# One-bank PSUM tiles, a sum moved past the meeting of the MLP halves, and accumulating output stores in a hybrid block on Trainium2

## The chip, the cores and the metric

The kernel runs on one core of one Trainium2 chip. Its time is the device time of one execution in microseconds; the median of three executions of the kernel before is 2062.95 us (2062.31 to 2064.06).

## The reference

One layer of a streaming encoder for 512 tokens of width 2048, in float32. Cut to what matters:

```python
h = rmsnorm(x, norm_mix_pre)
proj = h @ w_in                                  # 2048 -> 1024 + 4 * 1024: u, q, f, i, g
y_pool = pool_mixer(u, pool_w, pool_b, pool_scale)
y_hgrn = hgrn2_mixer(q, f, i, g, lb, hgrn_norm_w)    # gated linear recurrence, chunks of 64
mix = concatenate([y_pool, y_hgrn]) @ w_out      # 2048 -> 2048
x = x + rmsnorm(mix, norm_mix_post)
h = rmsnorm(x, norm_mlp_pre)
ff = square(relu(h @ w_mlp_in)) @ w_mlp_out      # 2048 -> 8192 -> 2048
x = x + rmsnorm(ff, norm_mlp_post)
```

## The kernel before

**Products.** Each float32 operand is split into a high part (a ScalarE cast to a shorter format, names with h: wh, mh) and a low part (a VectorE subtraction, names with l: wl, ml; lines L214, L215 for the projections' weights, L857, L858 for the MLP's, L1124, L1125 for its activations). Each product is three matmuls: high by high, high by low, low by high. A bank of PSUM holds 128 partitions by 512 float32; there are eight.

**Order.** The program is written out by hand. On each engine the instructions run in the order in which the Python code issues them; a pool of tiles or a data dependence adds a wait to an instruction, but nothing is reordered. Dependences in PSUM are kept by tile: where two banks are one tile, an instruction that writes the second bank is ordered behind one that reads the first.

**Input projection and w_out (L250).** The projection runs in ten groups, each filling four banks, and w_out in four groups (n = 0 to 3, 512 columns each) with the four row tiles of 128 tokens as its four banks. The depth of 2048 is done in four units; in the last unit each bank is finished in turn and then evicted, that is, read out of PSUM and scaled, by VectorE (pu L436, F L515, Q L534) or ScalarE (V L541, G L546); for w_out by ScalarE's square with a row sum (junk L810) and VectorE's product with a gain (Y L811). The recurrence runs between, in small pieces handed out by a clock of units; it uses the other four banks (pool pss). The residual task after w_out makes the rows x2 = x + rmsnorm(mix) of each row tile t, and stores them from POOL's queue into a DRAM buffer x2_dram.

**MLP.** It is a Strassen-type scheme: 16 groups g, each with seven products i in the order (1, 2, 5, 3, 6, 7, 4), and each product in two column blocks q: 14 slots in a group, 224 in all. Groups 0 to 7 are the in half (products_in: L1019 with 256 columns in g = 0, while the pool pss is still open and four banks are left; L1014 and L1015 after that, with eight). Slots of the in half are evicted by evac_in in two parts h: take (ScalarE copy L1052) and add (VectorE L1049, L1067) collect products in a buffer t, which finish_in multiplies by the row factor and squares (L1033, L1034) and stores to h_dram (L1035, POOL's queue). Groups 8 to 15 are the out half (products, L1208); evac_out adds each slot's bank pair to the rows YT (L1233).

**The meeting of the halves.** The activations of the out half are read back into r and combined: act_steps lists sums S (sum_a, L1132) and splits (split_a, L1124, L1125) with the slot before which each is to be ready, and run_pend pops them in this order, some in each slot. S and the buffers t of the last in group come from one pool tag, "tmp", with three buffers, so a new S waits until the store of an old t has read its buffer.

**Queues.** SP's queue carries plain weight loads, the loads of r, the residual rows xs and the output stores (L1260). POOL's queue carries the weight loads that accumulate two blocks into one tile (L864), the stores to h_dram and those of x2.

**End.** In the last group, d counts its 14 slots. At d = 4 the four row tiles of x2 are loaded back as xs. Slots with the last product of a column block are added (L1233), squared with a row sum (L1240, ScalarE), multiplied by the gain wpost (L1246, VectorE); finish_steps then makes y · rt + xs (L1258) for each row tile in three steps and stores it. Steps of the row tiles 0 and 1 are popped two per slot from d = 9 on; those of 2 and 3 stand in the last slot, which is evicted in two halves.

Of the kernel before, what the change touches and what calls it, by code (L numbers as in the profile page):

```python
# [28 lines left out]
def hybrid_block(  # L29
# [34 lines left out]
    psg = ctx.enter_context(tc.tile_pool(name="psg", bufs=2, space=PSUM))  # L64
# [699 lines left out]
    def residual_task(t):  # L764
# [10 lines left out]
        nc.gpsimd.dma_start(x2_dram[t * P:(t + 1) * P, :], Y[t])  # L775
# [182 lines left out]
    ps_in = [psg.tile([P, 2, 512], F32, tag="g", name=f"mi{k}") for k in range(2)]  # L958
    PA, PG = ps_in[0:1], ps_in[1:2]
# [38 lines left out]
    def products_in(k, hook):  # L998
# [9 lines left out]
        for n, (m, kt) in enumerate(mk):  # L1008
# [7 lines left out]
            else:  # L1016
                o = main[0][:, m // 2, (m % 2) * 256:(m % 2) * 256 + 256]
# [117 lines left out]
    def act_steps(p):  # L1135
# [7 lines left out]
            (0, 0, lambda: sum_a(1, None, r_block(1, 1), ALU.subtract)),  # L1143
# [22 lines left out]
    for k in range(n_in):  # L1166
# [21 lines left out]
        if k == 13:  # L1188
            assert "rbc2" in late
            pss_pool.__exit__(None, None, None)  # L1190
            psm = ctx.enter_context(tc.tile_pool(name="psm", bufs=1, space=PSUM, reuse_waits="tile"))
# [4 lines left out]
    al, ga = ps_mo, ps_in[::-1]

    def products(k):
# [6 lines left out]
        for h, kt in hk:  # L1205
            ts = slice(h * P, (h + 1) * P)
            for oi, (l, r) in enumerate(((0, hi), (0, lo), (1, hi))):
                nc.tensor.matmul(bank[:, h, :], a[:, l, kt, ts], r[:, kt, :],  # L1208
# [10 lines left out]
    def evac_out(k):  # L1219
# [10 lines left out]
        end = k == len(slots) - 1  # L1230
        parts = [slice(h, h + 1) for h in range(2)] if end else [slice(0, 2)]
        for hs in parts:
            nc.vector.tensor_tensor(out=yv[:, hs], in0=yv[:, hs], in1=bank[:, hs],  # L1233
                                    op=ALU.add if sign > 0 else ALU.subtract)
# [6 lines left out]
            if end:  # L1241
                yw = M["yw"][:, hs]
            else:
                yw = yv
# [1 line left out]
            nc.vector.tensor_tensor(out=yw if end else yw[:, hs], in0=yv[:, hs], in1=wp, op=ALU.mult)  # L1246
# [73 lines left out]
```

## Time and profile before

| | us |
|---|---|
| median of 3 runs | 2062.95 (2062.31 to 2064.06) |
| profiled execution | 2061.68 |
| its span | 2060.0 |
| PE busy | 1975.7 (96%) |
| VectorE busy | 1286.0 (62%) |
| ScalarE busy | 832.7 (40%) |
| POOL busy | 195.6 (9%) |
| HBM traffic | 326.14 MB read, 25.17 MB written, 171 GB/s |

The stages on the span: input projection with the recurrence until about 546 us, w_out until 745, the in half of the MLP until about 1430, the out half to the end. The page's rows name an engine, a line and "out<-in" tiles: pj are the projection's banks, om those of w_out, mi and mo those of the MLP. A bracket [0.79 <-DVE F L515] says that the engine had been idle for 0.79 us and that VectorE's F at L515 ended the wait.

### The profile page before, as it was taken

To read this page: it belongs to the slowest core of one execution; us is meant where nothing else is said; L and a number is where in the kernel's file an instruction comes from. 1 tells how busy PE (TensorE), PEld (TensorE's weight loads), DVE (VectorE), ACT (ScalarE), POOL (GpSimd) and SP (SyncE) were. 2 spreads that over 40 slices of the span, in tenths; PEclk is the share of its full clock that TensorE was granted. 3 is DMA by queue.
4 is the path that set the end of the run, shared out by engine and by line. 5 is a ranking of instruction groups with operands and counts; after the bars stand their busy time and mean duration, and the time that the engine had idled before them with its cause. 6 is when DMAs were issued, how large, how long until landed. Compare 5 with 4: busy or idle time off the path is not lost.

```text
span 2060.0 us, 24502 instructions
## 1 busy us (share of the span) xinstructions
PE 1975.7 (96%) x10066; PEld 1665.3 (81%) x10066; DVE 1286.0 (62%) x1392; ACT 832.7 (40%) x1009; POOL 195.6 (9%) x229
## 2 busy tenths in 40 slices
PE   9999999999989987999999999998999999999995
PEld 7778887888777777888888888887888888888884
DVE  4537533653632267566666656666778778778877
ACT  5322222222232255444444444445554444444443
POOL 1000000000000001011111111110110110110110
PEclk9999999999999998999999999999999999999998
DMA  5322123221243276798998998996998998998994
GB/s 193 104 82 82 62 82 98 68 80 62 93 183 102 82 215 112 213 206 210 209 215 211 216 212 215 217 245 172 252 222 205 236 222 213 222 227 219 224 241 127
DMA packets 165680, 352.90 MB, mean 171 GB/s; under 512 B 6008, under 2 KB 9152, under 8 KB 163776
## 3 DMA queue, kind: packets, MB, share of 16 engines
q0 software_dynamic: 73680, 160.47, 40.2%
q1 hardware_dynamic: 91888, 190.86, 27.1%
q8 instruction: 79, 1.29, 0.3%
q14 instruction: 33, 0.27, 0.0%
HBM read 326.14 MB, written 25.17 MB: 171 GB/s over the span
## 4 chain that ended last, share of the span: by engine, by line
PE 88%; DVE 5%; ACT 2%; issue 1%; DMA 0%; DVEq 0%; ACTq 0%; POOLq 0%
PE pj L250 20%; PE mo L1208 16%; PE mi L1208 13%; PE mi L1014 9%; PE om L250 8%; PE mo L1014 8%; PE mi L1015 5%; PE mo L1015 4%; PE mi L1019 3%; PE lps L600 2%; DVE ml L858 1%; DVE t L1049 1%; ACT mh L857 0%; DVE YT L1258 0%; PE po L663 0%
## 5 line engine op out<-in xcount | busy, mean ns | idle before, releaser
L1014 PE MATMUL mi<-a,mh 128*128 128x512 f32 x896 | 316.5, 398 | 11.9 <-DVE t L1049 11.9
L1208 PE MATMUL mo<-mh,o 128*128 128x512 f32 x1024 | 318.5, 391 | 1.1 <-ACT mh L857 1.1
L250 PE MATMUL pj<-xT,wh 128*128 128x512 f32 x768 | 243.3, 397 | 10.9 <-DVE pu L436 3.8
L858 DVE TENSOR_TENSOR ml<-X,mh 128x1024 fp32r<-128x1024 f32 x176 | 207.4, 1220 | 70.3 <-ACT mh L857 70.3
L1015 PE MATMUL mi<-a,ml 128*128 128x256 f32 x896 | 251.1, 280 | 0.0
L857 ACT CAST mh<-X 128x1024 fp32r<-128x1024 f32 x176 | 179.7, 1050 | 167.8 <-PE mo L1014 53.4
L1208 PE MATMUL mi<-mh,o 128*128 128x512 f32 x768 | 237.7, 389 | 0.0
L858 DVE TENSOR_TENSOR ml<-YX,mh 128x1024 fp32r<-128x1024 f32 x176 | 207.4, 1220 | 46.1 <-ACT mh L857 46.1
L857 ACT CAST mh<-YX 128x1024 fp32r<-128x1024 f32 x176 | 180.1, 1051 | 137.8 <-PE mo L1208 48.0
L1014 PE MATMUL mo<-a,mh 128*128 128x512 f32 x672 | 235.2, 395 | 0.0
L1208 PEld LDWEIGHTS mo<-mh,o 128*128 128x128 f32 x1024 | 192.9, 188 | 42.2 <-ACT mh L857 2.2
L215 DVE TENSOR_TENSOR wl<-wr,wh 128x1024 fp32r<-128x1024 f32 (+1 forms) x116 | 136.2, 1186 | 132.8 <-ACT wh L214 132.6
L1014 PEld LDWEIGHTS mi<-a,mh 128*128 128x128 f32 x896 | 169.3, 189 | 53.7 <-ACT mh L857 7.3
L1208 PE MATMUL mo<-ml,o 128*128 128x512 f32 x512 | 200.3, 391 | 6.4 <-DVE ml L858 6.4
L1015 PE MATMUL mo<-a,ml 128*128 128x256 f32 x672 | 187.5, 279 | 0.0
L250 PEld LDWEIGHTS pj<-xT,wh 128*128 128x128 f32 x768 | 142.0, 189 | 45.4 <-DVE pu L436 5.5
L214 ACT CAST wh<-wr 128x1024 fp32r<-128x1024 f32 (+1 forms) x116 | 115.3, 1016 | 156.4 <-PE pj L250 81.8
L250 PE MATMUL pj<-wh,xT 128*128 128x512 f32 x512 | 170.0, 398 | 3.1 <-ACT G L546 3.1
L1015 PEld LDWEIGHTS mi<-a,ml 128*128 128x128 f32 x896 | 170.0, 190 | 0.0
L1208 PEld LDWEIGHTS mi<-mh,o 128*128 128x128 f32 x768 | 144.1, 188 | 29.9
L250 PE MATMUL pj<-xT,wl 128*128 128x512 f32 x384 | 150.5, 392 | 0.0
L1014 PEld LDWEIGHTS mo<-a,mh 128*128 128x128 f32 x672 | 126.1, 188 | 30.0
(222 smaller groups left out, 3033.0 us busy)
## 6 DMA issues: line engine op xcount, KB each, us to landing
wr<-in_w_in SPq DMA_DIRECT2D x39, 1024.0 KB, 5.2
X<-in_w_mlp_in POOLq DMA_DIRECT2D x33, 1024.0 KB, 8.7
X<-in_w_mlp_out POOLq DMA_DIRECT2D x33, 1024.0 KB, 9.8
YX<-in_w_mlp_in POOLq DMA_DIRECT2D x23, 1024.0 KB, 9.8
YX<-in_w_mlp_out POOLq DMA_DIRECT2D x23, 1024.0 KB, 9.8
YX<-in_w_mlp_in SPq DMA_DIRECT2D x21, 1024.0 KB, 5.4
YX<-in_w_mlp_out SPq DMA_DIRECT2D x21, 1024.0 KB, 5.1
wr<-in_w_out SPq DMA_DIRECT2D x16, 1024.0 KB, 5.1
```

The lines of the kernel that those rows point to most:

```text
L214: nc.scalar.copy(out=hi[:, ks, :], in_=raw[:, ks, :])
L215: nc.vector.tensor_tensor(out=lo[:, ks, :], in0=raw[:, ks, :], in1=hi[:, ks, :].bitcast(F32), op=ALU.subtract)
L250: nc.tensor.matmul(bank, l, r, start=first and kt == 0 and oi == 0, stop=last and kt == 3 and oi == 2)
L600: nc.tensor.matmul(ps[r:r + mb, h, w, b0:b1], K[:, h, w * P + r:w * P + r + mb], rhs[:, b0:b1, 1, :], start=True, stop=True)
L857: nc.scalar.copy(out=hi[:, ks, :], in_=raw[:, ks, :])
L858: nc.vector.tensor_tensor(out=lo[:, ks, :], in0=raw[:, ks, :], in1=hi[:, ks, :].bitcast(F32), op=ALU.subtract)
L1014: nc.tensor.matmul(o, hi[:, kt, ms], r, start=st, stop=False, skip_group_check=True)
L1015: nc.tensor.matmul(o[:, 0], lo[:, kt, ms], r[:, 0], start=False, stop=sp, skip_group_check=True)
L1019: nc.tensor.matmul(o, l[:, kt, ms], r[:, x], start=st and oi == 0 and m % 2 == 0, stop=sp and oi == 2, skip_group_check=True)
L1049: nc.vector.tensor_tensor(out=t, in0=t, in1=half(banks, s_), op=sign)
L1208: nc.tensor.matmul(bank[:, h, :], a[:, l, kt, ts], r[:, kt, :], start=i in (1, 2, 5) and kt == 0 and oi == 0, stop=kt == 3 and oi == 2, sk ...
```

## The change

Four edits.

1. The pool psg gives four tiles of one bank instead of two of two banks. This holds for the projection, w_out and the first group of the MLP (g = 0).
2. When the recurrence's pool closes (slot 13), psg closes with it and a new pool psm takes all eight banks as four two-bank tiles; at the meeting psm closes, and a pool pso takes them as al0, ga0, ga1 (two banks each) and al1 as two one-bank tiles. A slot in al1 (i in 1, 6, 7, 4 with q = 1) is evicted by two operations of 512 columns instead of one of 1024.
3. For the first out group (p = 0) the sum S1 may run only from the end of the in half on (14 instead of 0 in the table of act_steps); the entries behind it follow, since the list is popped in order.
4. The rows x2 of the row tiles 0 and 1 are stored to the output itself instead of x2_dram. They are not loaded again; their finish is y · rt · wpost (one operation, 1024 columns each time) and a store from POOL's queue that accumulates into the output. The separate product with wpost goes for them. Their four steps are popped at d = 10, 11 and 12 and, the last, inside the last slot between its two halves.

The core of the diff:

```diff
-    psg = ctx.enter_context(tc.tile_pool(name="psg", bufs=2, space=PSUM))
+    psg_pool = tc.tile_pool(name="psg", bufs=4, space=PSUM)
+    psg = psg_pool.__enter__()
...
     def new_banks(name):
-        g = [psg.tile([P, 2, 512], F32, tag="g", name=f"{name}_{j}") for j in range(2)]
-        return [g[j // 2][:, j % 2] for j in range(4)]
+        return [psg.tile([P, 512], F32, tag="g", name=f"{name}_{j}") for j in range(4)]
...
-        nc.gpsimd.dma_start(x2_dram[t * P:(t + 1) * P, :], Y[t])
+        nc.gpsimd.dma_start((out2d if t < 2 else x2_dram)[t * P:(t + 1) * P, :], Y[t])
...
-    ps_in = [psg.tile([P, 2, 512], F32, tag="g", name=f"mi{k}") for k in range(2)]
-    PA, PG = ps_in[0:1], ps_in[1:2]
+    ps_in = [psg.tile([P, 512], F32, tag="g", name=f"mi{k}") for k in range(4)]
+    PA, PG = ps_in[0:2], ps_in[2:4]
...
-                o = main[0][:, m // 2, (m % 2) * 256:(m % 2) * 256 + 256]
+                o = main[m // 2][:, (m % 2) * 256:(m % 2) * 256 + 256]
...
-            (0, 0, lambda: sum_a(1, None, r_block(1, 1), ALU.subtract)),
+            (0, 0 if p else 14, lambda: sum_a(1, None, r_block(1, 1), ALU.subtract)),
...
             pss_pool.__exit__(None, None, None)
-            psm = ctx.enter_context(tc.tile_pool(name="psm", bufs=1, space=PSUM, reuse_waits="tile"))
-            ps_mo = [psm.tile([P, 2, 512], F32, name=f"mo{q}") for q in range(2)]
-            PA, PG = ps_in[::-1], ps_mo
+            psg_pool.__exit__(None, None, None)
+            psm_pool = tc.tile_pool(name="psm", bufs=1, space=PSUM, reuse_waits="tile")
+            psm = psm_pool.__enter__()
+            ps_in = [psm.tile([P, 2, 512], F32, name=f"ps{q}") for q in range(4)]
+            PA, PG = ps_in[2:4], ps_in[0:2]
     while ends:
         ends.pop(0)()
-    al, ga = ps_mo, ps_in[::-1]
+    psm_pool.__exit__(None, None, None)
+    pso = ctx.enter_context(tc.tile_pool(name="pso", bufs=1, space=PSUM, reuse_waits="tile"))
+    al = [pso.tile([P, 2, 512], F32, name="al0")] + [[pso.tile([P, 512], F32, name=f"al1{h}") for h in range(2)]]
+    ga = [pso.tile([P, 2, 512], F32, name=f"ga{q}") for q in range(2)]
...
-        parts = [slice(h, h + 1) for h in range(2)] if end else [slice(0, 2)]
-        for hs in parts:
-            nc.vector.tensor_tensor(out=yv[:, hs], in0=yv[:, hs], in1=bank[:, hs],
-                                    op=ALU.add if sign > 0 else ALU.subtract)
+        op = ALU.add if sign > 0 else ALU.subtract
+        for hs in [slice(h, h + 1) for h in range(2)] if type(bank) is list else [slice(0, 2)]:
+            src = bank[hs.start].unsqueeze(1) if type(bank) is list else bank
+            if g == NP and i in FIRST:
+                nc.scalar.copy(out=yv[:, hs], in_=src)
+                continue
+            nc.vector.tensor_tensor(out=yv[:, hs], in0=yv[:, hs], in1=src, op=op)
...
-            wp = M["wpost"][:, cs].unsqueeze(1).to_broadcast([P, hs.stop - hs.start, 512])
-            nc.vector.tensor_tensor(out=yw if end else yw[:, hs], in0=yv[:, hs], in1=wp, op=ALU.mult)
+            if tp == 2:
+                yw = M["yw"][:, hs] if end else yv[:, hs]
+                wp = M["wpost"][:, cs].unsqueeze(1).to_broadcast([P, hs.stop - hs.start, 512])
+                nc.vector.tensor_tensor(out=yw, in0=yv[:, hs], in1=wp, op=ALU.mult)
             if end:
                 for f in finish_steps(2 + hs.start):
                     f()
+                while steps:
+                    steps.pop(0)()
...
+            if t < 2:
+                nc.vector.scalar_tensor_tensor(out=y[:, c0:c1], in0=y[:, c0:c1], scalar=rt[0],
+                                               in1=M["wpost"][:, c0:c1], op0=ALU.mult, op1=ALU.mult)
+                nc.gpsimd.dma_start(out2d[rows, c0:c1], y[:, c0:c1], accum_op=ALU.add)
+                return
...
-            xa, xb = M["r"], M["12"].bitcast(F32)
-            for t in range(4):
-                load_xs(t, flat((xa if t < 2 else xb)[:, t % 2]))
+            for t in (2, 3):
+                load_xs(t, flat(M["r"][:, t % 2]))
...
-        for _ in range(2):
-            if steps and d < 13:
-                steps.pop(0)()
+        elif 10 <= d <= 12:
+            steps.pop(0)()
```

How the order moves. First TensorE in the last unit of w_out's group n = 0, from the last matmul of the first row tile's bank into the second's; wh and wl are the split weights, mp the split activations, and om_0 before is the tile that holds the banks of the row tiles 0 and 1. Before:

```order
L250 MATMUL om_0_3552<-wh_3720,mp_3675 128x512 [waits Activation_49]
L250 MATMUL om_0_3552<-wl_3721,mp_3675 128x512
L250 MATMUL om_0_3552<-wh_3720,mp_3675 128x512 [waits DVE_49] x2
L250 MATMUL om_0_3552<-wl_3721,mp_3675 128x512
L250 MATMUL om_0_3552<-wh_3720,mp_3675 128x512 x2
```

And now:

```order
L251 MATMUL om_0_3572<-wh_3742,mp_3697 128x512 [waits Activation_49]
L251 MATMUL om_0_3572<-wl_3743,mp_3697 128x512
L251 MATMUL om_0_3572<-wh_3742,mp_3697 128x512 [waits DVE_49]
L251 MATMUL om_1_3573<-wh_3742,mp_3697 128x512
L251 MATMUL om_1_3573<-wl_3743,mp_3697 128x512
L251 MATMUL om_1_3573<-wh_3742,mp_3697 128x512 x2
```

Before, two matmuls with a wait for VectorE stand side by side: the last of the first bank, and the first of the second bank. Now the second bank is a tile of its own, om_1, and its first matmul has no wait.

VectorE at the meeting of the halves; t_ is the buffer of a product of the last in group (t_9389, t_9228, t_9565 before; t_9422, t_9261, t_9593 now), S_9457 or S_9656 the sum S1, ml a low part of split weights. Before:

```order
L1033 SCALAR_TENSOR_TENSOR t_9389<-t_9389,rbc 128x1024 [waits DVE_49]
L1132 TENSOR_TENSOR S_9457<-S_9366,r 128x1024 [waits DMASW4_49,Activation_49]
L858 TENSOR_TENSOR ml_4644<-YX,mh_4643 128x1024 [waits DMASW2_49,PE_49,Activation_49]
L858 TENSOR_TENSOR ml_4644<-YX,mh_4643 128x1024 [waits PE_49,Activation_49]
L1049 TENSOR_TENSOR t_9228<-t_9228,mi_4685 128x512 [waits PE_49]
```

And now:

```order
L1033 SCALAR_TENSOR_TENSOR t_9422<-t_9422,rbc 128x1024 [waits DVE_49]
L858 TENSOR_TENSOR ml_4672<-YX,mh_4671 128x1024 [waits DMASW2_49,PE_49,Activation_49]
L858 TENSOR_TENSOR ml_4672<-YX,mh_4671 128x1024 [waits PE_49,Activation_49]
L1049 TENSOR_TENSOR t_9261<-t_9261,ps_5662 128x512 [waits PE_49]
...
L1033 SCALAR_TENSOR_TENSOR t_9593<-t_9593,rbc 128x1024 [waits DVE_49]
L858 TENSOR_TENSOR ml_4711<-YX,mh_4710 128x1024 [waits DMAHW2_49,Activation_49]
L858 TENSOR_TENSOR ml_4711<-YX,mh_4710 128x1024 [waits Activation_49]
L1132 TENSOR_TENSOR S_9656<-S_9399,r 128x1024 [waits DMASW5_49]
```

S1, with its wait for a DMA, stood between the finish of one t and the additions to the next; it now stands behind the finish of the last t.

VectorE in the last two slots; YT_9328 before and YT_9361 now hold the row tiles 0 and 1, YT_9416 and YT_9449 the tiles 2 and 3, YX the gain wpost. Before:

```order
L858 TENSOR_TENSOR ml_4683<-X_4470,mh_4682 128x1024 x2
L1233 TENSOR_TENSOR YT_9416<-YT_9416,mo_5629 128x2x512
L1246 TENSOR_TENSOR YT_9416<-YT_9416,YX 128x2x512
L1233 TENSOR_TENSOR YT_9416<-YT_9416,mo_5630 128x512
L1246 TENSOR_TENSOR yw<-YT_9416,YX 128x512
```

And now, from the same add of slot d = 12:

```order
L1239 TENSOR_TENSOR YT_9449<-YT_9449,al_9622 128x2x512
L1249 TENSOR_TENSOR YT_9449<-YT_9449,YX 128x2x512
L753 TENSOR_REDUCE sst<-ss_m 128x1
L134 TENSOR_SCALAR msq<-sst 128x1
L756 RECIPROCAL rt_y<-rt_y 128x1
L757 SCALAR_TENSOR_TENSOR rt<-rt_y,msq 128x1
L758 SCALAR_TENSOR_TENSOR rt<-rt,rt_y 128x1
L1264 SCALAR_TENSOR_TENSOR YT_9361<-YT_9361,rt,YX 128x1024
L1239 TENSOR_TENSOR YT_9449<-YT_9449,al_9623 128x512
L1249 TENSOR_TENSOR yw<-YT_9449,YX 128x512
```

The beginning of row tile 1's finish, its row factor (L753 to L758) and its first 1024 columns, stood two slots earlier before; it now stands between the last full eviction and the first half of the last slot. Its second 1024 columns stand still later, between the two halves of the last slot.

More of the change, by code (lines that the diff above doesn't have):

```diff
@@ L1042, in half @@
             if s_ is None:
-                return banks[0][:, h].rearrange("p (a b) -> p a b", a=2)
+                return banks[h].rearrange("p (a b) -> p a b", a=2)
             return banks[h][:, :, s_ * 256:(s_ + 1) * 256]
@@ L1207, in products @@
             for oi, (l, r) in enumerate(((0, hi), (0, lo), (1, hi))):
-                nc.tensor.matmul(bank[:, h, :], a[:, l, kt, ts], r[:, kt, :],
+                nc.tensor.matmul(bank[h] if type(bank) is list else bank[:, h, :], a[:, l, kt, ts], r[:, kt, :],
                                  start=i in (1, 2, 5) and kt == 0 and oi == 0,
@@ L1225, in evac_out @@
         yv = M["y1" if tp == 1 else "y2"][:, :, cs]
-        if g == NP and i in FIRST:
-            nc.scalar.copy(out=yv, in_=bank)
-            return
         final = g == 2 * NP - 1 and i in LAST
         end = k == len(slots) - 1
-        parts = [slice(h, h + 1) for h in range(2)] if end else [slice(0, 2)]
-        for hs in parts:
-            nc.vector.tensor_tensor(out=yv[:, hs], in0=yv[:, hs], in1=bank[:, hs],
-                                    op=ALU.add if sign > 0 else ALU.subtract)
+        op = ALU.add if sign > 0 else ALU.subtract
[5 more added lines that the diff above has]
+            nc.vector.tensor_tensor(out=yv[:, hs], in0=yv[:, hs], in1=src, op=op)
             if not final:
@@ L1240, in evac_out @@
                 nc.scalar.activation(out=junk, in_=yv[:, h], func=AF.Square, accum_out=ss_m[:, t, n:n + 1])
[L1241 to L1244, printed above, removed]
-            wp = M["wpost"][:, cs].unsqueeze(1).to_broadcast([P, hs.stop - hs.start, 512])
-            nc.vector.tensor_tensor(out=yw if end else yw[:, hs], in0=yv[:, hs], in1=wp, op=ALU.mult)
+            if tp == 2:
+                yw = M["yw"][:, hs] if end else yv[:, hs]
+                wp = M["wpost"][:, cs].unsqueeze(1).to_broadcast([P, hs.stop - hs.start, 512])
+                nc.vector.tensor_tensor(out=yw, in0=yv[:, hs], in1=wp, op=ALU.mult)
             if end:
@@ L1254, in finish_steps, with begin @@
         y = y_rows(t)
+        rows = slice(t * P, (t + 1) * P)
         def part(c0, c1):
-            src = M["yw"][:, t % 2] if t >= 2 and c0 == 1024 else y[:, c0:c1]
+            if t < 2:
[3 more added lines that the diff above has]
+                return
+            src = M["yw"][:, t % 2] if c0 == 1024 else y[:, c0:c1]
             nc.vector.scalar_tensor_tensor(out=y[:, c0:c1], in0=src, scalar=rt[0], in1=M["xs", t][:, c0:c1],
                                            op0=ALU.mult, op1=ALU.add)
-            nc.sync.dma_start(out2d[t * P:(t + 1) * P, c0:c1], y[:, c0:c1])
-        return [lambda: (rt.append(row_rstd(t)), part(0, 1024)), lambda: part(1024, 1536), lambda: part(1536, 2048)]
+            nc.sync.dma_start(out2d[rows, c0:c1], y[:, c0:c1])
+        def begin():
+            rt.append(row_rstd(t))
+            part(0, 1024)
+        if t < 2:
+            return [begin, lambda: part(1024, 2048)]
+        return [begin, lambda: part(1024, 1536), lambda: part(1536, 2048)]
     def load_xs(t, tl):
```

## The prediction

> **What bounds the kernel now.** I read the page's busy shares and its chain of waits first, then TensorE's waits by releaser, then a table of the span by stage, then the timeline at the waits that are worth something.
>
> ```profile
> span 2060.0 us, 24502 instructions
> PE 1975.7 (96%) x10066; PEld 1665.3 (81%) x10066; DVE 1286.0 (62%) x1392; ACT 832.7 (40%) x1009; POOL 195.6 (9%) x229
> PE 88%; DVE 5%; ACT 2%; issue 1%; DMA 0%; DVEq 0%; ACTq 0%; POOLq 0%
> ```
>
> TensorE is busy for 96% of the span and carries 88% of the chain that ended last. No matmul is added or dropped, so what can be had is its idle time, 2060.0 − 1975.7 = 84.3 us, and the time in which it runs below full clock. The next view says who ends the idle time: total us, times, longest.
>
> ```profile
> PE mi L1014 <- DVE t L1049: 11.9, 7, 6.3
> PE om L250 <- DVE Y L811: 11.7, 6, 4.0
> PE mi L1019 <- ACT t L1052: 10.3, 6, 4.5
> PE mi L1019 <- DVE t L1049: 7.1, 4, 4.6
> ...
> PE pj L250 <- DVE pu L436: 3.8, 4, 1.5
> PE pj L250 <- DVE F L515: 3.1, 4, 0.8
> PE pj L250 <- ACT G L546: 3.1, 4, 0.8
> PE pj L250 <- DVE Q L534: 2.2, 4, 0.8
> PE om L250 <- DVE sst L753: 2.2, 2, 1.5
> ```
>
> These are evictions: TensorE waits until VectorE or ScalarE has read PSUM. The stages where time is lost, and one where none is (start and end, length, busy PE, weight loads, VectorE, ScalarE, POOL, granted clock):
>
> ```profile
> 745.00:800.00 55.00, 40.46 (x314) 39.00 (x312) 42.45 (x48) 34.63 (x60) 7.56 (x7) 0.92 0.70 172
> 800.00:860.00 60.00, 54.25 (x403) 52.49 (x404) 34.98 (x39) 25.34 (x29) 6.79 (x7) 0.93 0.74 186
> 1400.00:1440.00 40.00, 32.35 (x152) 26.76 (x151) 25.83 (x26) 19.98 (x22) 4.28 (x5) 0.91 0.61 164
> 1750.00:2000.00 250.00, 249.93 (x1103) 206.61 (x1103) 199.78 (x174) 120.82 (x122) 35.38 (x28) 1.00 0.94 228
> 2000.00:2060.00 60.00, 39.27 (x161) 30.72 (x159) 42.65 (x59) 18.98 (x38) 2.53 (x2) 0.87 0.56 138
> ```
>
> These are the first group of the MLP's in half (745 to 860), the meeting of the halves, a stretch of the out half, where TensorE is full, and the tail.
>
> **One-bank tiles in the input projection and w_out.** Before, two banks are one tile: the first matmul of its second bank waits until the first bank, finished a moment ago, has been read out. That falls twice in each group of four banks; in the changed order neither matmul has such a wait.
>
> ```profile
> 111.65 0.61 PE L250 MATMUL pj<-xT,wh 128*128 128x512 f32 x2
> 112.33 0.61 PE L250 MATMUL pj<-xT,wh 128*128 128x512 f32 x2
> ...
> 113.95 0.74 PE L250 MATMUL pj<-xT,wh 128*128 128x512 f32 x2 [0.79 <-DVE F L515]
> 590.80 0.80 PE L250 MATMUL om<-wh,mp 128*128 128x512 f32 x1 [3.95 <-DVE Y L811]
> 591.82 1.06 PE L250 MATMUL om<-wh,mp 128*128 128x512 f32 x2
> 593.10 0.94 PE L250 MATMUL om<-wh,mp 128*128 128x512 f32 x2
> ```
>
> Triples of matmuls start 0.68 us apart (111.65 to 112.33). The triple due at 113.01 starts at 113.95, 0.94 late, and its first two matmuls take 0.74 instead of 0.61: 1.07 lost where the view shows 0.79, so each wait costs 0.28 more than it shows. The four projection rows hold 3.8 + 3.1 + 3.1 + 2.2 = 12.2 us in 16 waits, 16.7 with 16 × 0.28. One wait is twice as long as the others (1.5), so something else is late there as well: I leave it out and take **15.2**, bounds 12.2 and 16.7. In w_out the rows hold 11.7 + 2.2 = 13.9 in 8 waits; 8 × 0.28 adds 2.2, and behind the wait of 3.95 triples start 1.28 apart (591.82 to 593.10) for some 1.5 us lost: 17.6. In the last group ScalarE's squares pace the evictions, so I take **16.8**; the lower bound is 8, if most of the long wait only moves to the next group. What hides the evictions now: a bank is written again only after three other banks' matmuls.
>
> **The first MLP group.** The same dependence runs through two-bank tiles here, and evictions stand in VectorE's queue behind work that prepares the MLP's activations.
>
> ```profile
> 774.25 0.40 PE L1019 MATMUL mi<-a,mh 128*128 128x256 f32 x2
> 774.61 0.40 PE L1019 MATMUL mi<-a,mh 128*128 128x256 f32 x2
> 780.62 0.80 PE L1019 MATMUL mi<-a,mh 128*128 128x256 f32 x2 [4.61 <-DVE t L1049]
> 781.42 0.63 PE L1019 MATMUL mi<-a,mh 128*128 128x256 f32 x2
> 782.06 0.63 PE L1019 MATMUL mi<-a,mh 128*128 128x256 f32 x2
> 799.89 0.79 PE L1019 MATMUL mi<-a,mh 128*128 128x256 f32 x2 [4.52 <-ACT t L1052]
> 829.38 0.80 PE L1019 MATMUL mi<-a,mh 128*128 128x256 f32 x2 [2.07 <-ACT t L1052]
> ```
>
> The two L1019 rows hold 10.3 + 7.1 = 17.4. Behind the waits of 4.61, 4.52 and 2.07 triples start 0.64 apart (781.42 to 782.06) instead of 0.36 (774.25 to 774.61); with some six such triples each, 3 × 6 × 0.28 = 5.0. All of it would be 22.4. But matmuls that come sooner need their split activations and weights sooner, from a VectorE that is busy 42.45 of the 55 us. When I take the waits out of the order and let VectorE's and ScalarE's queues run on at their own durations, new waits for split operands give back about 6: **16**. Bounds: 8, if the split chain holds the two longest waits, and 22.4.
>
> [...]
>
> **The meeting of the halves.** The sum S takes a buffer that a store still reads. VectorE waits for it, and the four additions that TensorE needs stand behind it.
>
> ```profile
> 1406.08 1.23 DVE L1132 TENSOR_TENSOR S<-S,r 128x1024 f32<-128x1024 f32 x1 [5.32 <-DMA h_dram<-t]
> ...
> 1409.50 2.72 DVE L1049 TENSOR_TENSOR t<-t,mi 128x512 f32<-128x512 f32 x4
> 1411.04 0.77 PE L1014 MATMUL mi<-a,mh 128*128 128x512 f32 x1 [6.32 <-DVE t L1049]
> ```
>
> The change puts this S, and what is queued behind it, after the last two tiles of the half. The wait of 6.32 goes. The granted clock of 0.91 over 32.35 busy us makes up to 2.9 of slowness; I count 2.4. What is late next are splits made from S, pieces of 1.23 that the order puts up to one slot later: 0.5 given back, so **8.2**, bounds 5 and 9.
>
> **The out half.** One of four banks is now read by two 512-column operations instead of one of 1024: 4 in each of 8 groups, 32 in all. By the rows of the next fence a 1024 operation takes its successor 1.14 us to follow (2011.86 to 2013.00) and a 512 one lasts 0.69: 2 × 0.69 − 1.14 = 0.24 more, 7.7 us in all. In 250 us VectorE is busy 199.78; a slot (112 of them in some 560 us) is 5.0 us and has 1.0 of slack. The loads of two row tiles that go from SP's queue and the x2 rows that land in the output instead lie beside a full TensorE too. **Nothing**, while the slack lasts.
>
> [...]
>
> **The tail**, from the timeline, and from the DMA issues (KB each, us to landing).
>
> ```profile
> 2011.86 1.23 DVE L1246 TENSOR_TENSOR YT<-YT,YX 128x1024 f32<-128x1024 f32 x1 [1.40 <-ACT junk L1240]
> 2013.00 2.35 DVE L858 TENSOR_TENSOR ml<-YZ,mh 128x1024 fp32r<-128x1024 f32 x2
> 2032.51 0.50 PE L1208 MATMUL mo<-ml,o 128*128 128x512 f32 x1 [1.67 <-DVE ml L858]
> 2045.47 0.69 DVE L1233 TENSOR_TENSOR YT<-YT,mo 128x512 f32<-128x512 f32 x1 [0.65 <-PE mo L1208]
> 2055.27 0.74 DVE L1258 SCALAR_TENSOR_TENSOR YT<-YT,rt,o 128x512 f32<-128x512 f32 x1
> X<-in_w_mlp_out POOLq DMA_DIRECT2D x33, 1024.0 KB, 9.8
> out<-YT SPq DMA_DIRECT2D x4, 512.0 KB, 2.7
> ```
>
> VectorE sets the end: from 2011.86 on it stops only for ScalarE's squares (1.40). Four multiplications by the gain (1.23) go there, two adds are halved, and one finishing step of the second tile moves between the halves of the last slot, behind the last matmul but ahead of the last eviction. Laying the changed order out at these durations, with TensorE's waits for splits, VectorE ends 1.05 us earlier: **1**. As bounds I take 2 gained and, if the moved step (1.2) and a later store end the kernel, 3 lost. The four accumulating stores are absent before. The last is issued some 9 us before the end: with the plain store's 2.7 it is hidden; with 9.8, of the nearest accumulating transfer, twice as large, it just about is. I take it as hidden.
>
> **The sum.** 15.2 + 16.8 + 16 + 8.2 + 1 = 57.2. The profiled execution took 2061.68 us (its span and 1.68): 2004.5. The median of the three runs is 1.27 above it: **2006**. The upper bounds give 16.7 + 17.6 + 22.4 + 9 + 2 = 67.7, 1995; the lower ones 12.2 + 8 + 8 + 5 − 3 = 30.2, 2033.
>
> **Rivals.** *The evictions were only the last of several.* Where VectorE and ScalarE are late themselves, TensorE waits for the next thing they owe. For it: 42.45 of 55 us in the first group, and a wait of 3.95 that is longer than any eviction. Against it: the projection's waits of 0.8 are an eviction's own length. Gain: projection 15.2, w_out 8, first group 8, meeting 5, tail 0 = 36, **2027**.
>
> *The stores end last.* If the third and fourth accumulating store, some 6 us apart, go one after the other at 9.8 each, the fourth starts 3.8 after its issue and lands 13.6 after it; issued 9 before the end, it lands 4.6 past it: 57.2 − 4.6, **2010**. Against it: these stores are half as large.
>
> *VectorE becomes the bound of the out half.* Place: the 32 halved evictions. Price: the row at 2032.51, a matmul that waits 1.67 for a late split, with 0.28 of refill 1.95; 32 × 1.95 = 62, less the 57 gained: **2068**, slower. It decides from the point where a slot asks VectorE for over 5.0 us; it asks for 4.0 now and 4.2 then in the mean, so only slots with sums and splits of activations together come near.
>
> *The one-bank tiles do nothing*, because each wait comes back at the next group's first write of the bank. Against it: the order has that wait three banks later. Then 8.2 + 1 is left: **2054**.
>
> **How the numbers follow.** The forecast gets 0.61, the first rival 0.20, the stores 0.10, VectorE's bound 0.04, tiles without effect 0.03, and 0.02 goes to no change at all. This kernel's measurement can tell about 0.2%, 4 us, from no change. Faster: 0.61 + 0.20 + 0.10 + 0.03 = 0.94; within: 0.02; slower: 0.04. The range takes in the forecast's own bounds but for its far end, the first rival and the stores: 1995 to 2030.
>
> **What would show it.** Right: no waits of L251 on F, G, Q, pu or Y; the stretch from the w_out stage's end to the first group's end shorter by about 16 with a clock near 1; no wait of S on h_dram; TensorE idle of some 35 us. Wrong: the same waits with another releaser (mh, ml, a) in the first group; TensorE idle in the out half; an end that follows the last arithmetic by over 4 us.

## The result

The changed kernel takes 2004.97 us (median of four runs, 2002.77 to 2008.68) against 2063.24 (2062.31 to 2064.06): 0.972 of the time before, 95% interval 0.9702 to 0.9737, 58.3 us less. The prediction was 2006, with 1995 to 2030. The profiled execution took 2002.77 us. Its page:

```profile
span 2001.0 us, 24529 instructions
PE 1958.5 (98%) x10066; PEld 1660.9 (83%) x10066; DVE 1283.9 (64%) x1416; ACT 832.5 (42%) x1011; POOL 199.0 (10%) x233
PE 92%; DVE 4%; ACT 2%; issue 1%; DMA 0%; SPq 0%; DVEq 0%; ACTq 0%
```

The same 10066 matmuls, and TensorE idle for 2001.0 − 1958.5 = 42.5 us where it was 84.3. The other 17 us of the gain are busy time, 1975.7 to 1958.5: matmuls that were slower before. Some ran at a lower granted clock (0.91 to 0.93 in the first MLP group and at the meeting), others stood right behind a short wait, as the projection's pairs of 0.74 in place of 0.61, where the window 112.30:115.70 shows a clock of 1.00. TensorE's waits by releaser (total us, times, longest), the first five rows:

```profile
PE ps L1014 <- DVE t L1049: 7.3, 7, 2.0
PE mi L1019 <- DVE a L890: 2.9, 3, 1.8
PE al L1213 <- DVE ml L858: 2.3, 3, 1.7
PE mi L1019 <- ACT t L1052: 1.8, 1, 1.8
PE mi L1019 <- DVE t L1049: 1.8, 1, 1.8
```

No eviction ends a wait of pj or om any more; what pj still waits for is its operand xT, 1.7 us in three waits (1.8 before). In the first MLP group two of ten waits for evictions are left. Where a stage begins is read from the views of four places in which TensorE's matmuls are issued; each row ends with the first and the last start. Before:

```profile
L250 PE MATMUL om<-wh,mh x256: 389/389/501, 545.9 to 741.1; 128*128 128x512 f32 x128
L1019 PE MATMUL mi<-a,mh x448: 278/283/682, 744.8 to 860.6; 128*128 128x256 f32 x150
L1014 PE MATMUL mi<-a,mh x896: 391/395/766, 860.9 to 1424.3; 128*128 128x512 f32 x180
L1208 PE MATMUL mo<-mh,o x1024: 387/389/628, 1424.7 to 2045.0; 128*128 128x512 f32 x171
```

And of the changed kernel:

```profile
L251 PE MATMUL om<-wh,mh x256: 389/389/476, 528.9 to 706.4; 128*128 128x512 f32 x128
L1019 PE MATMUL mi<-a,mh x448: 274/283/682, 711.1 to 809.7; 128*128 128x256 f32 x150
L1014 PE MATMUL ps<-a,mh x1568: 390/395/473, 810.0 to 1366.8; 128*128 128x512 f32 x196
L1213 PE MATMUL al<-mh,o x1024: 387/389/632, 1367.2 to 1981.6; 128*128 128x512 f32 x171
```

The differences of these marks, and of the two spans at the end, put the gain where the prediction's terms can be held against it:

| stretch | before | after | gain | term of the sum |
|---|---|---|---|---|
| start to first om | 545.9 | 528.9 | 17.0 | 15.2 |
| to first L1019 (w_out) | 198.9 | 182.2 | 16.7 | 16.8 |
| to first L1014 (first MLP group) | 116.1 | 98.9 | 17.2 | 16 |
| to first out matmul (rest of the in half, meeting) | 563.8 | 557.2 | 6.6 | 8.2 |
| to the last matmuls (out half) | 620.3 | 614.4 | 5.9 | 1, both rows |
| to the end of the span | 15.0 | 19.4 | −4.4 | |
| together | 2060.0 | 2001.0 | 59.0 | 57.2 |

Not all of the 5.9 belongs to the tail. 1.6 of it lies ahead of slot d = 8: from the first out matmul to VectorE's addition of that slot, which in both kernels had waited 1.95 for TensorE, it is 2009.24 − 1424.7 = 584.5 before and 1950.10 − 1367.2 = 582.9 now.

```profile
2009.24 1.22 DVE L1233 TENSOR_TENSOR YT<-YT,mo 128x1024 f32<-128x1024 f32 x1 [1.95 <-PE mo L1208]
1950.10 1.22 DVE L1239 TENSOR_TENSOR YT<-YT,al 128x1024 f32<-128x1024 f32 x1 [1.95 <-PE al L1213]
```

Most of this stands right behind the meeting, in two waits of the kernel before that are a single one of 0.27 now (at 1373.28):

```profile
1430.87 0.49 PE L1208 MATMUL mo<-mh,o 128*128 128x512 f32 x1 [0.57 <-ACT mh L857]
1432.13 0.50 PE L1208 MATMUL mo<-ml,o 128*128 128x512 f32 x1 [0.76 <-DVE ml L858]
```

The windows of the changed kernel, with the columns that the prediction explained (and, last, the busy share of the DMA engines and GB/s), show the clock and what VectorE is asked:

```profile
711.00:760.00 49.00, 42.11 (x341) 40.72 (x342) 43.47 (x49) 35.30 (x62) 7.56 (x7) 1.00 0.80 195
760.00:810.00 50.00, 48.19 (x385) 47.50 (x384) 33.87 (x38) 24.64 (x28) 6.79 (x7) 0.97 0.88 221
1385.00:1700.00 315.00, 315.00 (x1391) 260.84 (x1390) 250.17 (x230) 156.57 (x155) 42.98 (x34) 1.00 0.94 226
1945.00:2001.00 56.00, 34.76 (x143) 27.39 (x141) 38.10 (x56) 17.70 (x37) 4.67 (x5) 0.84 0.62 123
```

In the first MLP group the clock is 1.00 and 0.97 where it was 0.92 and 0.93, and VectorE is now busy for 43.47 of 49 us. At the end the arithmetic and the stores read, from the timeline:

```profile
1988.89 1.28 DVE L1264 SCALAR_TENSOR_TENSOR YT<-YT,rt,YX 128x1024 f32<-128x1024 f32 x1
1990.09 0.68 DVE L1239 TENSOR_TENSOR YT<-YT,al 128x512 f32<-128x512 f32 x1
1994.64 0.75 DVE L1269 SCALAR_TENSOR_TENSOR YT<-YT,rt,r 128x512 f32<-128x512 f32 x1
1990.47 0.84 POOL L1266 DMA_DIRECT2D out<-YT  x1 [5.59 <-DVE YT L1264]
```

VectorE ends at 1994.64 + 0.75 = 1995.4, 628.2 us behind the first out matmul where it was 2056.0 − 1424.7 = 631.3: 3.1 earlier, of which 1.6 is the part ahead of d = 8. From d = 8's addition to VectorE's end it is 45.3 us, where it was 46.8: 1.5 earlier. But from its end to the span's end it is 5.6 us, where it was 4.0. The DMA issues (count, KB, median us to landing) say why:

```profile
out<-YT POOLq DMA_DIRECT2D x4, 512.0 KB, 5.7
out<-YT SPq DMA_DIRECT2D x2, 512.0 KB, 4.1
out<-YT SPq DMA_DIRECT2D x4, 256.0 KB, 4.3
```

Before, the plain stores landed in 2.7 (512 KB) and 2.8 us (256 KB); now, with the last accumulating store issued at 1990.47 beside them, those of the row tiles 2 and 3 take 4.1 and 4.3. All of the tail's 1.5 goes back there.

### The profile page after: what moved, and what is told of

Its sections match the earlier page's. It is cut to its first block, busy times and chain, and to the rows that moved or that the text cites. A ratio compares the mean times of both kernels' runs of the same rounds, so it can differ in the third digit from the quotient of the medians.

```text
span 2001.0 us, 24529 instructions
## 1 busy us (share of the span) xinstructions
PE 1958.5 (98%) x10066; PEld 1660.9 (83%) x10066; DVE 1283.9 (64%) x1416; ACT 832.5 (42%) x1011; POOL 199.0 (10%) x233
## 4 chain that ended last, share of the span: by engine, by line
PE 92%; DVE 4%; ACT 2%; issue 1%; DMA 0%; SPq 0%; DVEq 0%; ACTq 0%
PE pj L251 21%; PE ps L1014 18%; PE al L1213 16%; PE ga L1213 13%; PE ps L1015 9%; PE om L251 8%; PE mi L1019 3%; PE lps L600 2%; DVE ml L858 1%; DVE t L1049 1%; ACT junk L393 0%; ACT mh L857 0%; DVE a L890 0%; PE po L663 0%; ACT junk L1245 0%
## 5 line engine op out<-in xcount | busy, mean ns | idle before, releaser
L1014 PE MATMUL ps<-a,mh 128*128 128x512 f32 x1568 | 549.1, 395 | 7.3 <-DVE t L1049 7.3
L1015 PE MATMUL ps<-a,ml 128*128 128x256 f32 x1568 | 439.0, 280 | 0.0
L1014 PEld LDWEIGHTS ps<-a,mh 128*128 128x128 f32 x1568 | 293.9, 187 | 77.9 <-ACT mh L857 9.4
L1213 PE MATMUL al<-mh,o 128*128 128x512 f32 x1024 | 318.2, 390 | 0.2 <-ACT mh L857 0.2
L1015 PEld LDWEIGHTS ps<-a,ml 128*128 128x128 f32 x1568 | 296.0, 189 | 0.1
L857 ACT CAST mh<-X 128x1024 fp32r<-128x1024 f32 x176 | 179.6, 1049 | 159.4 <-PE ps L1014 53.4
L1213 PE MATMUL ga<-mh,o 128*128 128x512 f32 x768 | 237.7, 389 | 0.0
L857 ACT CAST mh<-YX 128x1024 fp32r<-128x1024 f32 x176 | 180.2, 1051 | 133.6 <-PE ga L1213 44.0
L1213 PEld LDWEIGHTS al<-mh,o 128*128 128x128 f32 x1024 | 192.9, 188 | 40.7 <-ACT mh L857 0.6
L1213 PE MATMUL al<-ml,o 128*128 128x512 f32 x512 | 200.2, 391 | 2.3 <-DVE ml L858 2.3
L1213 PEld LDWEIGHTS ga<-mh,o 128*128 128x128 f32 x768 | 144.1, 188 | 29.9
L1213 PE MATMUL ga<-ml,o 128*128 128x512 f32 x384 | 149.4, 389 | 0.0
L857 ACT CAST mh<-YZ 128x1024 fp32r<-128x1024 f32 x96 | 97.9, 1048 | 86.8 <-PE al L1213 41.7
```

What stands on the lines that cost most here:

```text
L857: nc.scalar.copy(out=hi[:, ks, :], in_=raw[:, ks, :])
L1014: nc.tensor.matmul(o, hi[:, kt, ms], r, start=st, stop=False, skip_group_check=True)
L1015: nc.tensor.matmul(o[:, 0], lo[:, kt, ms], r[:, 0], start=False, stop=sp, skip_group_check=True)
L1213: nc.tensor.matmul(bank[h] if type(bank) is list else bank[:, h, :], a[:, l, kt, ts], r[:, kt, :], start=i in (1, 2, 5) and kt == 0 and oi ...
```

## The experiments

Comparisons are with runs of the kernel before on the same chip, medians 2063.5 to 2064.7. The changed kernel's own four runs lie 6 us apart, so a difference of 2 us to it isn't told from none. It was timed for the result alone, not beside the experiments.

**One-bank tiles alone**, with the sum, the out half's banks and the tail as before:

```diff
-            (0, 0 if p else 14, lambda: sum_a(1, None, r_block(1, 1), ALU.subtract)),
+            (0, 0, lambda: sum_a(1, None, r_block(1, 1), ALU.subtract)),
...
-    al = [pso.tile([P, 2, 512], F32, name="al0")] + [[pso.tile([P, 512], F32, name=f"al1{h}") for h in range(2)]]
+    al = [pso.tile([P, 2, 512], F32, name=f"al{q}") for q in range(2)]
... (evac_out, finish_steps and the last loop as before)
```

> The kernel before with one-bank tiles in the projection, w_out and the first MLP group (and the four-tile pool that this needs afterwards), but with the sum S1, the out half's two-bank banks and the tail as before. Theory: the three stage gains of the full change, 17.0 (projection), 16.7 (w_out) and 17.2 (first group) by the marks of the two traces, stand alone: 50.9 us less than before, 2012; the wait of S on a store (5.3 on VectorE, 6.3 on TensorE) is still there. Rival, the gains need the other edits too (weights that come sooner, a VectorE freed elsewhere): 20 to 35 less, 2028 to 2043.

Measured: 2013.43 against 2063.54 (0.9761, interval 0.9746 to 0.9775), 50.1 less. The three stage gains stand alone, and they are 50.1 of the 58.3. Its longest wait is the one at the meeting, 6.4 where it was 6.3:

```profile
PE ps L1014 <- DVE t L1049: 11.7, 7, 6.4
```

**The first MLP group back on two-bank tiles**, all else as changed. The pool psg is closed and opened again for this; that needs its place behind pss and PA, PG exchanged later.

```diff
-    ps_in = [psg.tile([P, 512], F32, tag="g", name=f"mi{k}") for k in range(4)]
-    PA, PG = ps_in[0:2], ps_in[2:4]
+    psg_pool.__exit__(None, None, None)
+    psg_pool = tc.tile_pool(name="psg2", bufs=1, space=PSUM)
+    psg2 = psg_pool.__enter__()
+    ps_in = [psg2.tile([P, 2, 512], F32, name=f"mi{k}") for k in range(2)]
+    PA, PG = [[b[:, j] for j in range(2)] for b in ps_in]
```

> The changed kernel with the first MLP group alone put back on two-bank tiles (same four banks). Theory: the dependence by tile is the cause there; the stretch from the first L1019 to the first L1014 grows from 98.9 to 116 us again, and the time to about 2022, with waits of over 4 us behind evictions and triples at 0.64 behind them. Rival, the stretch was short of something else (weights, activations) that comes sooner now because the stages ahead end sooner or later: it stays under 105 and the time under 2012.

Measured: 2022.19 against 2063.54 (0.9801, 0.9786 to 0.9815), 17.2 above the changed kernel's 2004.97. By the marks the stage is 826.3 − 714.3 = 112.0 long, 13.1 more than the changed kernel's and not the whole of the 116 expected; 2.9 more lie just ahead of it. The lines have moved by three; waits and one window:

```profile
PE mi L1022 <- ACT t L1055: 10.3, 6, 4.5
PE mi L1022 <- DVE t L1052: 7.1, 4, 4.6
PE mi L1022 <- DVE Y L811: 3.7, 1, 3.7
```

```profile
711.00:828.00 117.00, 96.25 (x732) 93.41 (x733) 77.67 (x86) 62.01 (x93) 14.37 (x14) 0.94 0.74 180
```

The first two rows are, to the tenth, those of the kernel before: 10.3 and 7.1. So the dependence within a two-bank tile is what they were made of, whatever the stages ahead do. The third row belongs to the pool that is opened anew, and lies ahead of the stage, in the 2.9. The waits for split operands that the changed kernel has in this group, several small ones, are gone, which fits a stage short of 116.

**The sum alone**, in the kernel before:

```diff
-            (0, 0, lambda: sum_a(1, None, r_block(1, 1), ALU.subtract)),
+            (0, 0 if p else 14, lambda: sum_a(1, None, r_block(1, 1), ALU.subtract)),
```

> The kernel before with S1, and what is queued behind it, held to the end of the in half, and nothing else. Theory: the wait of 6.3 at the meeting goes and with it the slow pairs behind it; the stage from the first L1014 to the first L1208 shrinks by 6.6 as in the full change: 2056. Rival, the wait moves to the next store or to the splits that S feeds, so that 0 to 3 are left: 2060 to 2063.

Measured: 2056.02 against 2063.54 (0.9965, 0.9953 to 0.9976), 7.5 less. From the first L1014 to the first L1208 it is 557.0, 6.8 less; from there to the addition of d = 8 it is 583.2, 1.3 less, with a single wait of 0.25 behind the meeting. So these 1.3 come from the sum too. The wait at the meeting doesn't move on; it shrinks to 2.0:

```profile
PE mi L1014 <- DVE t L1049: 7.6, 7, 2.0
1400.00:1440.00 40.00, 37.74 (x191) 31.71 (x190) 30.26 (x30) 21.28 (x24) 4.29 (x5) 1.00 0.75 205
```

The clock of this window is 1.00; it was 0.91.

**The tail alone**, in the kernel before (edit 4 with two-bank tiles, the last slot by halves as before):

```diff
-        nc.gpsimd.dma_start(x2_dram[t * P:(t + 1) * P, :], Y[t])
+        nc.gpsimd.dma_start((out2d if t < 2 else x2_dram)[t * P:(t + 1) * P, :], Y[t])
... (evac_out, finish_steps and the last loop as changed, but for)
+        for hs in [slice(h, h + 1) for h in range(2)] if end else [slice(0, 2)]:
+            src = bank[:, hs]
```

> The kernel before with the first two row tiles ended by accumulating stores, and nothing else. Theory: VectorE's last stretch loses four products (1.2 each) but takes a step of 1.3 into the last slot, and the last stores land 1.6 later beside the accumulating ones; together within 2 us of before, 2061 to 2065. Rival one, the edit is worth its four products, 4 to 5 us: 2058. Rival two, the accumulating stores end last: over 2066.

Measured: 2062.24 against 2063.54 (0.9992, 0.9983 to 1.0002): no change that can be told: 1.3 less by the medians, with an interval that takes in none. In its trace VectorE ends 631.4 us behind the first out matmul, as before. With the two runs above, 50.1 + 7.5 + 1.3 = 58.9 beside 58.3 together: the edits add up as nearly as this scatter can show.

**The bank pair al1 as one tile**:

```diff
-    al = [pso.tile([P, 2, 512], F32, name="al0")] + [[pso.tile([P, 512], F32, name=f"al1{h}") for h in range(2)]]
+    al = [pso.tile([P, 2, 512], F32, name=f"al{q}") for q in range(2)]
```

> The changed kernel with the bank pair al1 of the out half as one two-bank tile again, read by one operation of 1024 columns (the last slot by halves, as before). Theory: the 32 halved evictions cost VectorE 0.24 each under cover of its slack, so the time stays within 2 us of the changed kernel's 2005. Rival, the halved evictions gain, since the first half is read while the second is being computed: 2008 to 2012. Rival, they cost TensorE: under 2002.

Measured: 2006.54 (2005.91 to 2008.9). **All eight banks one by one**, the opposite:

```diff
-    al = [pso.tile([P, 2, 512], F32, name="al0")] + [[pso.tile([P, 512], F32, name=f"al1{h}") for h in range(2)]]
-    ga = [pso.tile([P, 2, 512], F32, name=f"ga{q}") for q in range(2)]
+    al = [[pso.tile([P, 512], F32, name=f"al{q}{h}") for h in range(2)] for q in range(2)]
+    ga = [[pso.tile([P, 512], F32, name=f"ga{q}{h}") for h in range(2)] for q in range(2)]
```

> The changed kernel with all eight banks of the out half as one-bank tiles, so that each of its 112 slots, not 28 to 32 of them, is read by two operations of 512 columns. Theory: VectorE goes from about 4.1 us in a slot to 4.3 and stays under the slot's 5.0, TensorE stays full until the tail, and the tail loses about 1 us to shorter operations: 2005 to 2008. Rival, VectorE is the hidden bound of the out half: each added halving costs TensorE up to 1.95 us, over 2040.

Measured: 2004.98 (2004.49 to 2008.22). None, 32 or 112 halved evictions (the last slot aside) give 2006.5, 2005.0, 2005.0: within the scatter, the halving does nothing. What VectorE pays for it is covered.

**How much cover there is**: one or two more VectorE operations in each of the out half's first 98 slots. The buffer pad is read by nothing else.

```diff
+        if k < base:
+            nc.vector.tensor_tensor(out=pad, in0=pad, in1=pad, op=ALU.subtract)    # once or twice
```

> The changed kernel with one more VectorE operation of 1024 columns (1.14 us, on a buffer that nothing reads) in each of the out half's first 98 slots. Theory: with 4.1 + 1.14 = 5.3 us asked in a slot of 5.0 VectorE becomes the bound there: TensorE stalls on the low parts of the weights, 98 x 0.3 = 25 to 30 us, about 2032. Rival, the slack is larger than the busy time says (VectorE's waits are in front of its work, not free time): more than 50 us, over 2055; or smaller: within 5 us of 2005.

Measured with one: 2010.52 (2009.9 to 2011.08), 5.5 above the changed kernel, not 27.

> Two more VectorE operations of 1024 columns in each of the out half's first 98 slots, 2.28 us. The run with one of them cost 5.5 us where I had expected 27: the slot is 5.44 us by the changed kernel's chain (43.52 + 32.64 for 14 slots), not 5.0, and VectorE asks 4.0 of it by the windows (250.17 of 315), so 1.14 still went into the slack. Theory: 4.0 + 2.28 = 6.3 us is over 5.44, TensorE waits some 0.84 us in each of 98 slots, 82 us, about 2087. Rival, VectorE's work isn't what a slot waits for and its queue runs ahead: under 2030.

Measured with two: 2127.97 (2124.2 to 2129.78), 123 above it, not 82. The first expectation had the slot wrong, 5.0 for 5.44. The second had it right, but its 4.0 of work is still the busy share of a slot of 5.0: VectorE is busy for 250.17 of 315 us, 0.794 × 5.44 = 4.32. Then one operation asks 4.32 + 1.14 = 5.46 of 5.44, next to nothing over, and two ask 6.60, 1.16 over in each of 98 slots: 114. The two, which follow each other on one buffer, take 2.40 together and not 2.28 (from 1500.46 to the next addition at 1502.86; the changed kernel's two sums S, the second of which reads the first, take 2.39, from 1374.28 to 1376.67): 1.28 over, 125. Measured are 5.5 and 123. The windows, with one and then with two, show VectorE full, and the waits of the run with two show TensorE waiting for the low parts of the weights:

```profile
1385.00:1700.00 315.00, 312.99 (x1377) 258.08 (x1376) 308.78 (x286) 155.29 (x154) 40.45 (x32) 1.00 0.91 218
1385.00:1700.00 315.00, 278.00 (x1148) 212.73 (x1147) 312.25 (x283) 129.49 (x128) 35.40 (x28) 1.00 0.80 186
PE al L1213 <- DVE ml L858: 51.1, 55, 1.7
PE ga L1213 <- DVE ml L858: 21.1, 21, 1.9
```

So the third rival's point is measured: VectorE becomes the bound of the out half at some 1.1 us more in a slot, and a halved eviction asks 0.24 in one slot of four.

**A better tail** was tried in four ways, the first with all four row tiles ended by accumulating stores:

```diff
-        nc.gpsimd.dma_start((out2d if t < 2 else x2_dram)[t * P:(t + 1) * P, :], Y[t])
+        nc.gpsimd.dma_start(out2d[t * P:(t + 1) * P, :], Y[t])
... (no product with wpost, no xs; finish_steps takes its branch of t < 2 for every t)
```

> The changed kernel with all four row tiles ended by accumulating stores: no residual rows are loaded, and the product with the gain goes for the row tiles 2 and 3 as well. Theory: VectorE sets the end of the changed kernel, and it loses 5.2 us of products and 4.6 us of waits for squares in front of them; the last store, accumulating (0.84 to issue, 5.7 to land) instead of plain (4.3), gives 2.2 back: about 1997. Rival, the accumulating stores end last, one behind the other: 2001 to 2010.

Measured: 2008.2 (2007.33 to 2009.87), slower than the changed kernel if anything. The rival held. VectorE's last three operations began at 1991.77 and took 2.61, so arithmetic ended at 1994.4, 622.9 us behind the first out matmul (1371.5): 5.3 earlier than in the changed kernel, not the 9.8 that the expectation counted. The span ended 11.2 us later, where the changed kernel's ended 5.6 later: the stores took back 5.6. Timeline and DMA issues:

```profile
1991.77 2.61 DVE L1259 SCALAR_TENSOR_TENSOR YT<-YT,rt,YX 128x1024 f32<-128x1024 f32 x3
1993.35 2.58 POOL L1261 DMA_DIRECT2D out<-YT  x3 [2.98 <-DVE YT L1259]
out<-YT POOLq DMA_DIRECT2D x4, 256.0 KB, 8.1
```

Three issues of 0.86 one behind the other, and 8.1 to land, are the prediction's second rival in the one place where all stores come at the end.

The steps of the row tiles 0 and 1 put into VectorE's wait for the square, ahead of the product:

```diff
             if tp == 2:
+                if not end and steps and hs.start == 0:
+                    steps.pop(0)()
                 yw = M["yw"][:, hs] if end else yv[:, hs]
...
-        elif 10 <= d <= 12:
-            steps.pop(0)()
```

> The changed kernel with the steps of the row tiles 0 and 1 at d = 10, 11, 12 popped before the product with the gain instead of after it, into the time in which VectorE waits for ScalarE's square (1.47, 0.85 and 1.47 us). Theory: VectorE sets the end, so some 3.5 us go: 2001.5. Rival, the next low parts of the weights come later and TensorE's last matmul with them: 2004 to 2006.

Measured: 2002.77 (2002.1 to 2003.09) against 2063.91, 0.971 (0.9695 to 0.9724). That is the lowest median of all kernels here, and 2.2 below the changed kernel's, but it is also the changed kernel's fastest run, and the intervals of the two ratios overlap: it isn't told from it. In its trace VectorE ends 627.0 us behind the first out matmul, where it was 628.2: 1.2 earlier, not 3.5.

ScalarE to multiply by rt, with the product by the gain back in earlier slots:

```diff
-                nc.vector.scalar_tensor_tensor(out=y[:, c0:c1], in0=y[:, c0:c1], scalar=rt[0],
-                                               in1=M["wpost"][:, c0:c1], op0=ALU.mult, op1=ALU.mult)
+                nc.scalar.mul(y[:, c0:c1], src, rt[0])
```

> The changed kernel with another end for the row tiles 0 and 1: the product with the gain is back at their evictions (d up to 9, under a full TensorE), and rt is multiplied in by ScalarE at d = 10 and 11, between VectorE's addition and product, followed by the accumulating stores. Theory: VectorE loses four operations of 1.28 and the waits for the squares behind which the row factor's chain now stands, and the accumulating stores land before the last plain ones are issued: 5 to 7 us less, about 1999. Rival, ScalarE's casts of the next weights come later behind the new products: 2003 to 2006.

Measured: 2004.23 (2000.24 to 2006.71). The same with the row tile 2:

```diff
-            if t < 2:
+            if t < 3:
                 nc.scalar.mul(y[:, c0:c1], src, rt[0])
                 nc.gpsimd.dma_start(out2d[rows, c0:c1], y[:, c0:c1], accum_op=ALU.add)
```

> The run before this, and the row tile 2 too is ended by ScalarE and accumulating stores, in the last slot. Theory: VectorE's last 2.7 us of row tile 2 go to ScalarE, beside the second half's chain; another 2 us, about 1997. Rival, its three accumulating stores (0.84 each to issue, 6 to 8 to land) end last: 1999 to 2004.

Measured: 2004.26 (2001.83 to 2006.98). Neither is told from the changed kernel. The rival of the first shows in its waits: ScalarE's new products stand ahead of a cast of weights that TensorE then waits for.

```profile
PE al L1213 <- ACT mh L857: 2.2, 1, 2.2
```

## Why the prediction was right

**Projection and w_out.** 15.2 and 16.8 were forecast, 17.0 and 16.7 measured at the marks. The wait that I left out of the projection (1.5 long, because something else might be late there) went too: with it the term would have been 16.7. That each wait costs 0.28 more than the view shows is borne out by this sum: the shown waits alone would have been 12.2. The scatter doesn't undo this. In the traces of kernels with the same projection the first om starts at 545.9 to 546.2 with two-bank tiles and at 527.7 to 530.9 with one-bank tiles, at least 15.0 apart.

**First MLP group.** 16 forecast, 17.2 measured. The reading that VectorE's split chain would give some of it back was right in kind but only half of the 6 taken off. The waits for L890, a split of activations, grow from 0.9 to 2.9 us and one of 0.7 for a cast (L857) is new, some 2.8 in all with a small one; VectorE is the busier engine in the group's first half now (43.47 of 49). Another 3.6 stay because two evictions are still waited for, 1.8 each; the prediction had counted them as gone. That the two make 6.4, close to the 6, is luck. The lower bound of 8, and with it the first rival, needed the chain to hold the two longest waits; put back on two-bank tiles the group's waits return to the tenth, so they were the tiles' own.

**The meeting.** 8.2 forecast, 6.6 at the marks and 7.5 alone. What was mis-sized is what is late next. I had counted 0.5 for splits made from S. What is there is a wait of 2.0 for the same four additions: 6.3 − 2.0, and 2.4 for the clock, are the 6.7 at the place. VectorE's two splits of weights stand ahead of the additions and wait 2.07 for ScalarE's cast. The cast stands on ScalarE behind the square L1034, which itself waits for VectorE's product L1033:

```profile
1349.93 1.06 ACT L1034 ACTIVATE t<-t 128x1024 f32<-128x1024 f32 x1 [3.90 <-DVE t L1033]
1351.96 2.36 DVE L858 TENSOR_TENSOR ml<-YX,mh 128x1024 fp32r<-128x1024 f32 x2 [2.07 <-ACT mh L857]
1354.24 2.72 DVE L1049 TENSOR_TENSOR t<-t,ps 128x512 f32<-128x512 f32 x4
```

That cast was hidden in the 5.3 us for which VectorE waited for the store; it was never on the path before. Against this stand the waits of 0.57 and 0.76 behind the meeting, which went with the sum and which the prediction hadn't counted: with the 1.6 ahead of d = 8 the term is 8.2 after all. Two misses that cancel made it right.

**The out half.** For the halved evictions nothing was forecast and nothing was measured, but the slack was worked out of a slot of 5.0 us and 4.0 us of work, where 5.44 and 4.32 are right: I had divided 560 us by the 112 slots, and the out half takes 614. Both errors nearly cancel, 1.0 against 1.1.

**The tail.** 1 forecast. By the marks the last two rows give 1.5, but 1.6 of that is the meeting's, and nothing is left; alone the edit gave 1.3, which isn't told from none. VectorE ended 1.5 earlier where 1.05 was forecast, and the stores took back 1.6. I had taken the accumulating stores as hidden. They are, but the plain ones beside them land in 4.1 and 4.3 us instead of 2.7 and 2.8, which the prediction had no row for; its lower bound only allowed for a later store. One reading was wrong as well: of the four products with the gain only two stand behind 2011.86, where VectorE sets the end. The other two, at 1978.86 and 1984.96, lay under a full TensorE:

```profile
1984.96 1.23 DVE L1246 TENSOR_TENSOR YT<-YT,YX 128x1024 f32<-128x1024 f32 x1 [1.46 <-ACT junk L1240]
```

**The signs.** Of the signs of being right, the waits on evictions are gone, the first group is 17.2 shorter at a clock of 1.00 and 0.97, and S, now at 1374.28, waits for nothing; but TensorE is idle for 42.5 us, not some 35. Two signs of being wrong came in small: waits for a and mh in the first group, and an end 5.6 us behind the last arithmetic. The third didn't: TensorE is busy for all of the 315 us shown of the out half.

With the 1.6 put to the meeting, the errors of the terms, +1.8, −0.1, +1.2, 0.0 and −1.1, make the 1.8 between 57.2 and 59.0. The mechanism is right for all but the tail. That the median came out 1 us from the forecast owes something to errors that cancel, and a stage's length differs by up to 3 us between traces of the same instructions (the first group takes 98.9 to 101.6), so errors of this size aren't resolved.

## What to carry to other kernels

A dependence that is kept by tile makes two banks in one PSUM tile wait for each other's eviction, although no data pass between them (17.4 us of such waits in the first MLP group with two-bank tiles, 3.6 with one-bank tiles); where banks are evicted one at a time, the tile should be one bank (50.1 us less here), and the wait's price is its idle time, here some 0.28 us of slower matmuls behind it, and whatever it does to the clock (0.92 and 0.93 in that group before, 1.00 and 0.97 now). Price such a wait from the start times of the matmuls on both sides, not from the idle time alone. An accumulating store near the end cost 1.6 us here while plain stores ended last: they took 4.1 and 4.3 us to land in place of 2.7 and 2.8. Where it comes last itself, its issue and landing are the end: with all four row tiles ended so, three issues of 0.86 and 8.1 to land, and the span ended 11.2 us behind the last arithmetic.

## What the runs showed of the hardware that was not expected

The same idle time of TensorE, at the same place, was followed by full clock in one execution and by a lower one in another. At the meeting the changed kernel was idle for 2.00 us (start 1355.79) and the kernel with al1 as one tile for 2.06 (start 1357.16). The window around it, of the changed kernel first:

```profile
1340.00:1400.00 60.00, 57.73 (x287) 48.30 (x286) 46.15 (x45) 32.33 (x36) 6.99 (x8) 1.00 0.81 226
```

and of the other:

```profile
1340.00:1400.00 60.00, 57.69 (x282) 48.37 (x281) 44.86 (x44) 31.69 (x35) 6.83 (x7) 0.97 0.77 220
```

In the first the matmuls behind the wait take 0.40 us, in the second 0.63 from 1358.08 on; 0.03 of 57.7 busy us are an estimated 1.7 us from one wait. The stretch from the first L1014 to the first out matmul is 557.2 us in the first and 1370.1 − 810.1 = 560.0 in the second. The length of the wait alone doesn't decide it. Behind the longest wait of L1014 in the run with one more VectorE operation, 1.9, no matmul of that line takes over 0.47; behind 2.08 with all stores accumulating they go to 0.63, at a clock of 0.97 in the same window; and behind the 2.07 of the kernel before (829.38) matmuls of 256 columns take 0.41 instead of 0.28. In the tail single matmuls of the changed kernel take 0.63 behind 1.67 (1968.75), and those of the kernel before 0.40 and 0.39 behind the same 1.67 (2032.51). What decides it, no trace here shows. Part of the scatter between runs, 2002.77 to 2008.68 for the changed kernel and 2058.74 to 2067.89 for 15 of the kernel before on one chip, may come from this; that isn't shown, as most of them have no trace.

A plain store lands later beside an accumulating one: 2.7 to 2.8 us before, 4.1 to 4.3 with accumulating stores issued in the 12 us ahead (3.3 and 3.4 where the steps stand ahead of the product, with the last accumulating store issued at 1991.15). With ScalarE's products, where the four accumulating stores of the row tiles 0 and 1 are issued by 1984 and the plain ones from 1994 on, the plain ones take 2.7 and 2.9 again, and the span ends 4.0 us behind the last arithmetic, as before:

```profile
out<-YT SPq DMA_DIRECT2D x2, 512.0 KB, 2.7
out<-YT SPq DMA_DIRECT2D x4, 256.0 KB, 2.9
```
